# A scale for the value weights as a whole, the spatial product in float16 pairs, and masked key products evicted by another engine

## The chip, the cores and the metric

The kernel runs on one core of a Trainium2 chip. Its engines work through queues of their own: TensorE (PE: matmuls and transposes, with weight loads that overlap them), VectorE (DVE), ScalarE (ACT), GpSimd (POOL) and SyncE (SP, which here only issues DMAs). An engine takes its instructions in order and waits on semaphores for the others. Matmul results land in PSUM, of which there are eight banks, and are read from there by DVE or ACT. The metric is the device time of one execution in microseconds (us); lower is better.

## What is computed

One layer of a backbone with three parallel branches over 2048 + 128 tokens of width 1024. All inputs are float32. Cut to what the change touches:

```python
proj = einsum('btd,de->bte', xn, w_in)          # one projection, split into the branches' columns
# A: delta rule over chunks of 64 tokens
m = eye + beta[..., :, None] * einsum('bnhik,bnhjk->bnhij', k, k) * dec_strict
# B: spatial gating over chunks of 128 tokens, 4 groups of 128 channels
vn = rmsnorm(v, g_norm)                         # over 512 channels
vs = einsum('gpq,bnqgc->bnpgc', w_s, vn) + b_s  # w_s: (4, 128, 128)
o_b = u * vs * silu(z_b)
# C: Fourier mixing; then the branches' projections, sigmoid gates and the output projection
```

Here v is one of the column blocks of the projection, 512 wide, and the spatial product mixes the 128 tokens of a chunk within each group of channels.

## The kernel before

**Pairs of float16.** Almost every product is made from float16 pairs: an operand x with a scale s (a power of two) is kept as hi = f16(x s) and lo = f16(x s - hi), and the product is hi hi + hi lo + lo hi, three matmuls that add up in PSUM (`mm3`, `gemm_T`, `gemm_N`). ACT makes the high half, DVE the low one. The scale comes from a sum of squares: ACT squares and sums along a partition, a matmul with ones (`scales`) sums across partitions, and four one-column steps on DVE turn the sum's exponent into s and its inverse.

**Weights** are read by SP into one of two buffers (`wst`) and converted by a generator, `converting`, of which `weight_step` runs one step at each tick of the pacing object `pace`; `getw` takes the next weights of a list, `wlist`, and runs the remaining steps at once if they aren't done. The four column blocks of v have the tag "v" and fill one pair of tiles, `v4`; each block has its own scale and its own inverse.

**Order of the work.** After the input's normalisation come twelve tiles of the q, k and v columns of branch A (the loop over `ct`, line 610): matmuls over five token blocks, evicted by ACT into `raw`, a short convolution by three DVE instructions into `cy` (626 to 628), a SiLU by ACT and POOL (631, 632), and a store to DRAM (`qkv`, line 633). These tiles live in a pool `a1p`, which is closed behind the loop (639).

Then branch B begins (1131). It opens a pool `bp`, loads the bias `bsp`, transposes the spatial weights `wsn` into `wsT` (float32, line 1141), and runs over 17 blocks of 128 tokens (1159): 24 matmuls of xh, xl with `v4` into a bank of the PSUM pool `ps_mm` (three banks, in turn); line 1168 evicts it by DVE, with each block's inverse scale, into `vn` (a tile "sg" of the pool `ep`); ACT sums its squares into `vss` (1171, a tile of `bp`); DVE and POOL make the reciprocal root (170, 171); DVE scales `vn` by it (1177). One block later, `spatial` multiplies `vn` with `wsT` in float32, four groups into one bank of `ps_x` (two banks), and four DVE instructions (1151) apply the weight of the norm, which stands along partitions there (`sgug`), and add the bias. The result goes to DRAM and is read back by the loop over the gates (1191).

**Beside the branches** runs branch A's recurrence, a generator `delta` of which `pace.tick` runs a step after every so many microseconds of matmuls. Its first part, `prep` (677), makes for each of the 17 chunks the key product k k^T (729), and for both directions masks it: four DVE instructions per direction (735) multiply a head's 128x128 block in PSUM by beta and the decay. ACT copies the diagonal blocks (737) and makes the high half (739), DVE the low half (740). `base_inverse` (762) inverts the small diagonal blocks on DVE. All of `prep` reads what line 633 stored.

The instructions' order on each engine is set by a scheduler at build time, from the program's order and a timing model; dependences become semaphores.

Of the kernel before, what the change touches and what calls it, by code (L numbers as in the profile page):

```python
# [111 lines left out]
def hybrid_flow_kernel(ctx: ExitStack, tc: tile.TileContext, x_prompt, x_sample, state_delta, c, c_ctx, ln_g, w_ada,  # L112
# [85 lines left out]
    def converting(w, st, nkt, cols=P, hi=None, lo=None, tag="w", bufs=5):  # L198

        wpool = bwp[0] if tag == "b" else wp  # L200
        if tag == "z":
            hi, lo = [sb(p0p, [P, nkt, cols], n_, F16, bufs=4) for n_ in ("zhi", "zlo")]
        if tag == "v":
            hi, lo = [t[:, vfilled[0]] for t in v4]
            vfilled[0] += 1
        w.hi = sb(wpool, [P, nkt, cols], tag + "hi", F16, bufs=bufs) if hi is None else hi
        w.lo = sb(wpool, [P, nkt, cols], tag + "lo", F16, bufs=bufs) if lo is None else lo
        ss = sb(wp, [P, 1], "wss", bufs=4)
        A.activation(w.lo, st, AF.Square, accum_out=ss)  # L209
# [12 lines left out]
        A.activation(w.hi, st, AF.Copy, scale=s)  # L222
        V.scalar_tensor_tensor(w.lo, st, s, w.hi, ALU.mult, ALU.subtract)  # L223
# [33 lines left out]
    for c0 in ([C_QKV + i * P for i in range(12)] + [C_V + g * P for g in range(4)]  # L257
               + [x_ + g * P for g in range(4) for x_ in (C_U, C_ZB)] + [x_ + g * P for g in range(4) for x_ in (C_XC, C_ZC)]):
        wlist.append((w_in_[:, c0:c0 + P], KT, "v" if C_V <= c0 < C_V + WB else "w", 4))
# [4 lines left out]
    v4, vfilled = [], [0]  # L264
    goal = [0]
    wdone, wnext, wread, wlate, bwp, wsteps = [], [0], [], [0], [], []

# [340 lines left out]
    flip = [0]  # L608
    pace.start(decays(), 1.2)
    for ct in range(12):  # L610
        w = getw(1, 2 if ct < 6 else min(4, 15 - ct))
        for half in range(1):
            raw = sb(a1p, [P, LP], "raw")
            G.memset(raw[:, 0:1], 0.0)
            G.memset(raw[:, NS + 1:NS + 3], 0.0)
            G.memset(raw[:, LP - 1:LP], 0.0)
            for t0, tn in TBS:
                flip[0] ^= 1
                ps = bank(ps_d if flip[0] else ps_mm, [P, tn])
                gemm_T(ps, w, 0, xh[:, :, t0:t0 + tn], xl[:, :, t0:t0 + tn])  # L620
                o = t0 + 1 if t0 < NS else t0 + 3
                with tc.high_priority():
                    A.activation(raw[:, o:o + tn], ps, AF.Copy, scale=w.inv)
                pace.tick(tn / 100)
            y = sb(a1p, [P, LP - 2], "cy")
            V.tensor_scalar(y, raw[:, 0:LP - 2], convw(0, ct), None, ALU.mult)
            V.scalar_tensor_tensor(y, raw[:, 1:LP - 1], convw(1, ct), y, ALU.mult, ALU.add)
            V.scalar_tensor_tensor(y, raw[:, 2:LP], convw(2, ct), y, ALU.mult, ALU.add)
            for c0 in range(0, LP - 2, CQ):
                c1 = min(c0 + CQ, LP - 2)  # L630
                A.activation(raw[:, 1 + c0:1 + c1], y[:, c0:c1], AF.Sigmoid)  # L631
                G.tensor_tensor(y[:, c0:c1], y[:, c0:c1], raw[:, 1 + c0:1 + c1], ALU.mult)  # L632
            G.dma_start(qkvD[ct], y)
            if ct < 4 or ct > 7:
                A.activation(raw[:, 1:LP - 1], y, AF.Square, accum_out=vqs[:, ct:ct + 1])
# [41 lines left out]
    def prep(g, ci, t, nxt, held):  # L677
# [54 lines left out]
        for d in range(2):  # L732
            n_ = sb(d2, [P, WB], "n32", bufs=3)
            for h in range(H):
                V.scalar_tensor_tensor(n_[:, hs(h)], ps[:, hs(h)], beta[:, d, t, h:h + 1], dc[:, d, hs(h)], ALU.mult, ALU.mult)
# [3 lines left out]
            A.activation(n16[:, 0, :], n_, AF.Copy, scale=FS)  # L739
            V.scalar_tensor_tensor(n16[:, 1, :], n_, FS, n16[:, 0, :], ALU.mult, ALU.subtract)  # L740
            late(nD[d][t], n16)
            yield 1
# [390 lines left out]
    bp = pool(bs, "bp", 2)  # L1133
    bsp = sb(bp, [P, 4, P], "bsp", bufs=1)
    SY.dma_start(bsp, b_spatial[0].rearrange("g (o p) -> o g p", o=1).to_broadcast([P, 4, P]))
# [5 lines left out]
    V.tensor_copy(wsT, ps)  # L1141
    vinv = sb(ep, [P, 4], "vinv", bufs=1)
    for i in range(4):
        V.tensor_copy(vinv[:, i:i + 1], vw[i].inv)
    def spatial(t, vn):
        vs = sb(bp, [P, 4, P], "vs", bufs=4)
        ps = bank(ps_x, [P, 4, P])
        for g in range(4):
            mm(ps[:, g, :], vn[:, g, :], wsT[:, g, :])
        for g in range(4):  # L1150
            V.scalar_tensor_tensor(vs[:, g, :], ps[:, g, :], sgug(g), bsp[:, g, :], ALU.mult, ALU.add)
        vout.append((t, vs))

    def vstore():
# [4 lines left out]
    for t in range(NCH):  # L1159
        ps = bank(ps_mm, [P, 4, P])  # L1160
        ts = slice(t * P, (t + 1) * P)
        for k in range(KT):
            mm(ps, xh[:, k, ts], v4[0][:, :, k, :], k == 0, False)
            mm(ps, xh[:, k, ts], v4[1][:, :, k, :], False, False)
            mm(ps, xl[:, k, ts], v4[0][:, :, k, :], False, k == KT - 1)
        vn = sb(ep, [P, WB], "sg", bufs=4).rearrange("p (i c) -> p i c", i=4)
        with tc.high_priority():
            V.tensor_tensor(vn, ps, vinv.rearrange("p (i o) -> p i o", o=1).to_broadcast([P, 4, P]), ALU.mult)
        sq = sb(ep, [P, WB], "st", bufs=3)
        ss = sb(bp, [P, 1], "vss", bufs=3)  # L1170
        A.activation(sq, vn.rearrange("p i c -> p (i c)"), AF.Square, accum_out=ss)
        rsqrt(ss, ss, 1.0 / WB, 1)
        if vprev is not None:
            spatial(*vprev)
        if len(vout) > 2:
            vstore()
        V.tensor_scalar(vn, vn, ss, None, ALU.mult)
# [354 lines left out]
```

## Time and profile before

| | |
|---|---|
| time, median of 3 runs | 2209.3 us (2206.56 to 2211.78) |
| the profiled execution, first to last instruction | 2205.0 us |
| time around that span, by the median | 4.3 us |
| granted TensorE clock, mean | 0.993 |
| HBM read, written | 234.67 MB, 127.62 MB |

The profile is one execution; the page gives its span, and the median of the runs is 4.3 us above it. A row of instructions gives line, engine, operation, what is written and read, shape and count, then the busy time in us and the mean of one in ns, then the engine's idle time ahead of them and what ended it. A matmul's recorded duration holds its way through the array, so that the next one starts before it ends: what one costs is read from the distance of the starts. A row of stages gives the busy time of each engine within a window of the span. The granted clock is the share of full speed that the throttle gave TensorE.

### The profile page before, as it was taken

The page shows a single profiled execution, that of the slowest core. Times are in us where ns is not written, and L with a number is a line of the kernel's source. Part 1 is how long each engine was busy: PE and PEld are TensorE (multiplying, and loading weights), DVE is VectorE, ACT ScalarE, POOL GpSimd, SP SyncE. Part 2 cuts the span into 40 slices and gives each one's busy share as a digit, 9 for nine tenths or more (in the row PEclk, how much of TensorE's full clock was granted, in tenths as well). Part 3 has the DMA queues.
Part 4 walks back from the last instruction along what each step waited for, and adds up shares of the span by engine and source line. Part 5 has one row for each costly group of instructions (what it writes and reads, how often), then busy time and mean ns, then how long its engine had stood idle before and what let it go on. Part 6 is the DMA issues. An engine that isn't in the chain of part 4 may idle for free. (4 is left out here: it accounts for less than half of the span.)

```text
span 2205.0 us, 42035 instructions
## 1 busy us (share of the span) xinstructions
PE 2139.0 (97%) x15966; PEld 1233.8 (56%) x15966; DVE 1295.6 (59%) x3081; ACT 1007.0 (46%) x2322; POOL 704.9 (32%) x860
## 2 busy tenths in 40 slices
PE   7999999999999999999999999999999999999998
PEld 3564444456555588878555555556554444444443
DVE  5736954479889778255665555765674544223454
ACT  3644744445465464344644445665553422222332
POOL 1421333223343322432322223354542221122543
PEclk9999999999999999999999999999999999999999
DMA  8434823177786662443665555776664544324542
GB/s 280 143 96 147 287 94 107 63 210 221 232 245 221 203 186 88 116 122 114 220 182 162 163 167 183 238 212 213 193 197 151 168 127 131 117 77 125 170 149 103
DMA packets 304276, 365.05 MB, mean 166 GB/s; under 512 B 39393, under 2 KB 215626, under 8 KB 302026
## 3 DMA queue, kind: packets, MB, share of 16 engines
q1 hardware_dynamic: 288938, 302.19, 45.5%
q0 software_dynamic: 12688, 51.27, 6.4%
q10 hardware_dynamic: 2448, 8.91, 1.0%
q8 instruction: 125, 2.05, 0.4%
q14 instruction: 77, 0.63, 0.1%
HBM read 234.67 MB, written 127.62 MB: 164 GB/s over the span
## 5 line engine op out<-in xcount | busy, mean ns | idle before, releaser
L161 PE MATMUL b<-xh,whi 128*128 128x512 f16 (+1 forms) x1920 | 650.4, 347 | 3.2 <-DVE mrow L1361 1.2
L161 PE MATMUL b<-xl,whi 128*128 128x512 f16 (+1 forms) x1920 | 650.9, 347 | 0.0
L161 PE MATMUL b<-xh,wlo 128*128 128x512 f16 (+1 forms) x1920 | 650.4, 347 | 0.0
L161 PEld LDWEIGHTS <-whi 128*128 128x128 f16 x3904 | 358.1, 98 | 328.8 <-issue 7.9
L161 PEld LDWEIGHTS <-wlo 128*128 128x128 f16 x1952 | 191.3, 98 | 179.8 <-issue 2.4
L161 PE MATMUL b<-big,bhi 128*128 128x512 f16 (+1 forms) x960 | 251.6, 348 | 2.2 <-ACT big L1325 1.5
L1365 POOL TENSOR_TENSOR mrow<-mrow,sg 128x512 f32<-128x512 f32 (+1 forms) x80 | 91.9, 1149 | 296.5 <-DVE sg L1364 216.3
L161 PE MATMUL b<-big,blo 128*128 128x512 f16 (+1 forms) x480 | 163.7, 348 | 0.0
L1355 ACT ACTIVATE sg<-b,winv 128x512 f32<-128x512 f32 (+1 forms) x120 | 74.2, 618 | 170.5 <-PE b L161 169.6
L161 PEld LDWEIGHTS <-xh 128*128 128x128 f16 x1496 | 117.6, 98 | 30.2 <-issue 1.5
L161 PEld LDWEIGHTS <-bhi 128*128 128x128 f16 x960 | 86.7, 98 | 73.1 <-issue 2.7
L1364 DVE SCALAR_TENSOR_TENSOR sg<-b,binv,sg 128x512 f32<-128x512 f32 (+1 forms) x80 | 53.4, 668 | 125.2 <-PE b L161 118.1
L632 POOL TENSOR_TENSOR cy<-cy,raw 128x545 f32<-128x545 f32 (+1 forms) x48 | 66.9, 1421 | 183.4 <-ACT raw L631 183.4
L175 DVE CAST wscb<-wss 128x1 bf16<-128x1 f32 x93 | 14.3, 154 | 154.7 <-ACT wlo L209 65.8
L852 POOL COPY T<-ES 32x256 f16<-32x256 f16 x68 | 32.3, 475 | 207.1 <-DMA ES<-ei 168.2
L161 PE MATMUL b<-wlo,xh 128*128 128x128 f16 x544 | 92.9, 219 | 0.0
L161 PE MATMUL b<-whi,xh 128*128 128x128 f16 x544 | 92.9, 219 | 0.0
L161 PE MATMUL b<-whi,xl 128*128 128x128 f16 x544 | 92.9, 219 | 0.0
L161 PE MATMUL b<-wohi,mh 128*128 128x512 f16 x240 | 90.9, 379 | 1.3 <-ACT mh L1432 1.3
L161 PE MATMUL b<-wohi,ml 128*128 128x512 f16 x240 | 90.8, 379 | 0.3 <-DVE ml L1433 0.3
L161 PE MATMUL b<-wolo,mh 128*128 128x512 f16 x240 | 90.9, 379 | 0.0
L223 DVE SCALAR_TENSOR_TENSOR wlo<-wst,wsc,whi 128x1024 f16<-128x1024 f32 x52 | 70.4, 1358 | 30.8 <-ACT whi L222 30.7
(449 smaller groups left out, 4284.0 us busy)
## 6 DMA issues: line engine op xcount, KB each, us to landing
wst<-in_w_in_dram SPq DMA_DIRECT2D x60, 512.0 KB
qkv<-cy POOLq DMA_DIRECT2D x12, 1089.0 KB, 5.3
st<-br SPq DMA_DIRECT2D x48, 256.0 KB
mrow<-mrg SPq DMA_DIRECT2D x18, 512.0 KB
mrow<-mrg SPq DMA_DIRECT2D x16, 576.0 KB
mrg<-mrow POOLq DMA_DIRECT2D x16, 576.0 KB, 3.6
dc<-dec SPq DMA_DIRECT2D x17, 512.0 KB
kq<-qkv SPq DMA_DIRECT2D x34, 256.0 KB
```

The lines of the kernel that those rows point to most:

```text
L161: PE.matmul(out, l, r, start=start, stop=stop)
L175: V.tensor_copy(sb16, ss)
L223: V.scalar_tensor_tensor(w.lo, st, s, w.hi, ALU.mult, ALU.subtract)
L632: G.tensor_tensor(y[:, c0:c1], y[:, c0:c1], raw[:, 1 + c0:1 + c1], ALU.mult)
L852: G.tensor_copy(T16[rows(a0, b), :, :, b], ES[0:32, :, 2 * a0 + b, :, wT])
L1355: A.activation(sg, ps, AF.Sigmoid, scale=gw.inv)
L1364: V.scalar_tensor_tensor(sg, ps, binv[:, 1:2], sg, ALU.mult, ALU.mult)
L1365: G.tensor_tensor(mr, mr, sg, ALU.add)
```

## The change

In words, by part:

- **Value weights.** Each of the four blocks stands twice in the list. With tag "p" (a probe) it is read and its squares are summed into a column of `vsq`; after the fourth, one scale for all four is made. With tag "v" it is read again and converted with that scale. `getw` takes eight entries in place of four, and the convolution loop asks for more entries ahead (8 from tile 8 on).
- **Setup of branch B.** The weight of the norm is loaded as a row, `grow`, broadcast to all partitions, and multiplied by the inverse scale of v, by a scale for itself and by 1/64. `gss`, `grow`, `w16`, `einv` and `v16` are tiles of `bp`. The spatial weights become a float16 pair, `w16`, with a scale.
- **Eviction.** ACT squares and sums straight out of PSUM, with the inverse scale; DVE multiplies PSUM by `grow` into `vn`.
- **Product.** ACT and DVE make `vn` times the reciprocal root into a float16 pair, `v16`; the spatial product is three float16 matmuls per group; one DVE instruction over all four groups scales it and adds the bias. `vs` has three buffers in place of four.
- **Masked key products.** ACT evicts the four heads with beta as its scale, and one DVE multiplication over all heads applies the decay.

```diff
@@ converting
+        if tag == "p":
+            i = len(vprobed)
+            vprobed.append(i)
+            A.activation(v4[1][:, i], st, AF.Square, accum_out=vsq[:, i:i + 1])
+            yield
+            if i == 3:
+                V.tensor_reduce(vsq[:, 4:5], vsq[:, 0:4], AX.X, ALU.add)
+                vscale.extend(scales(vsq[:, 4:5], cp, "vsc"))
+                V.tensor_mul(vsq[:, 5:6], vscale[1], isx)
+            return
         if tag == "v":
             hi, lo = [t[:, vfilled[0]] for t in v4]
             vfilled[0] += 1
+            A.activation(hi, st, AF.Copy, scale=vscale[0])
+            V.scalar_tensor_tensor(lo, st, vscale[0], hi, ALU.mult, ALU.subtract)
+            return
@@ wlist
+    for tag in "pv":
+        for g in range(4):
+            wlist.append((w_in_[:, C_V + g * P:C_V + (g + 1) * P], KT, tag, 4))
@@ convolution loop
-        w = getw(1, 2 if ct < 6 else min(4, 15 - ct))
+        w = getw(1, 2 if ct < 6 else 4 if ct < 8 else 8)
@@ prep
             for h in range(H):
-                V.scalar_tensor_tensor(n_[:, hs(h)], ps[:, hs(h)], beta[:, d, t, h:h + 1], dc[:, d, hs(h)], ALU.mult, ALU.mult)
+                A.activation(n_[:, hs(h)], ps[:, hs(h)], AF.Copy, scale=beta[:, d, t, h:h + 1])
+            V.tensor_mul(n_, n_, dc[:, d, :])
@@ branch B
-    wsT = sb(bp, [P, 4, P], "wsT", bufs=1)
-    vw = getw(4, 3)
+    grow = sb(bp, [P, WB], "grow", bufs=1)
+    SY.dma_start(grow, sgu_norm_g.to_broadcast([P, WB]))
+    w16 = sb(bp, [P, 2, 4, P], "w16", F16, bufs=1)
+    vw = getw(8, 3)
+    gss = sb(bp, [P, 2], "gss", bufs=1)
+    junk = sb(ep, [P, WB], "sg", bufs=4)
+    A.activation(junk[:, 0:4], pc[:, 44:48], AF.Square, accum_out=gss[:, 0:1])
+    A.activation(junk, wsn.rearrange("p g q -> p (g q)"), AF.Square, accum_out=gss[:, 1:2])
+    sg_, ig_ = scales(gss[:, 0:1], bp, "gsc")
+    sw_, iw_ = scales(gss[:, 1:2], bp, "ssc")
+    vinv = vsq[:, 5:6]
+    V.tensor_scalar(grow, grow, vinv, sg_, ALU.mult, ALU.mult)
+    V.tensor_scalar(grow, grow, 1.0 / 64, None, ALU.mult)
+    einv = sb(bp, [P, 1], "einv", bufs=1)
+    V.scalar_tensor_tensor(einv, ig_, 64.0, iw_, ALU.mult, ALU.mult)
     ps = bank(ps_x, [P, 4, P])
     for g in range(4):
         PE.transpose(ps[:, g, :], wsn[:, g, :], ident)
-    V.tensor_copy(wsT, ps)
...
+    A.activation(w16[:, 0], ps, AF.Copy, scale=sw_)
+    V.scalar_tensor_tensor(w16[:, 1], ps, sw_, w16[:, 0], ALU.mult, ALU.subtract)
@@ spatial
         for g in range(4):
-            mm(ps[:, g, :], vn[:, g, :], wsT[:, g, :])
-        for g in range(4):
-            V.scalar_tensor_tensor(vs[:, g, :], ps[:, g, :], sgug(g), bsp[:, g, :], ALU.mult, ALU.add)
+            mm3(ps[:, g, :], [v16[:, l, g * P:(g + 1) * P] for l in range(2)], [w16[:, l, g, :] for l in range(2)])
+        V.scalar_tensor_tensor(vs, ps, einv, bsp, ALU.mult, ALU.add)
@@ loop over 17 blocks
         with tc.high_priority():
-            V.tensor_tensor(vn, ps, vinv.rearrange("p (i o) -> p i o", o=1).to_broadcast([P, 4, P]), ALU.mult)
...
-        A.activation(sq, vn.rearrange("p i c -> p (i c)"), AF.Square, accum_out=ss)
+            A.activation(sq, psf, AF.Square, scale=vinv, accum_out=ss)
+            V.tensor_mul(vn, psf, grow)
         rsqrt(ss, ss, 1.0 / WB, 1)
...
-        V.tensor_scalar(vn, vn, ss, None, ALU.mult)
-        vprev = (t, vn)
+        v16 = sb(bp, [P, 2, WB], "v16", F16)
+        A.activation(v16[:, 0, :], vn, AF.Copy, scale=ss)
+        V.scalar_tensor_tensor(v16[:, 1, :], vn, ss, v16[:, 0, :], ALU.mult, ALU.subtract)
+        vprev = (t, v16)
```

More of the change, by code (lines that the diff above doesn't have):

```diff
@@ L256, in hybrid_flow_kernel @@
         wlist.append((w_in_[:, c0:c0 + P], KT, "z", 4))
-    for c0 in ([C_QKV + i * P for i in range(12)] + [C_V + g * P for g in range(4)]
-               + [x_ + g * P for g in range(4) for x_ in (C_U, C_ZB)] + [x_ + g * P for g in range(4) for x_ in (C_XC, C_ZC)]):
-        wlist.append((w_in_[:, c0:c0 + P], KT, "v" if C_V <= c0 < C_V + WB else "w", 4))
+    for i in range(12):
+        wlist.append((w_in_[:, C_QKV + i * P:C_QKV + (i + 1) * P], KT, "w", 4))
+    for tag in "pv":
+        for g in range(4):
+            wlist.append((w_in_[:, C_V + g * P:C_V + (g + 1) * P], KT, tag, 4))
+    for c0 in ([x_ + g * P for g in range(4) for x_ in (C_U, C_ZB)] + [x_ + g * P for g in range(4) for x_ in (C_XC, C_ZC)]):
+        wlist.append((w_in_[:, c0:c0 + P], KT, "w", 4))
     for n in (1, 2, 0):
@@ L1140, in hybrid_flow_kernel, with spatial @@
         PE.transpose(ps[:, g, :], wsn[:, g, :], ident)
[L1141 to L1146, printed above, removed]
+    A.activation(w16[:, 0], ps, AF.Copy, scale=sw_)
+    V.scalar_tensor_tensor(w16[:, 1], ps, sw_, w16[:, 0], ALU.mult, ALU.subtract)
+    def spatial(t, v16):
+        vs = sb(bp, [P, 4, P], "vs", bufs=3)
         ps = bank(ps_x, [P, 4, P])
         for g in range(4):
-            mm(ps[:, g, :], vn[:, g, :], wsT[:, g, :])
-        for g in range(4):
-            V.scalar_tensor_tensor(vs[:, g, :], ps[:, g, :], sgug(g), bsp[:, g, :], ALU.mult, ALU.add)
+            mm3(ps[:, g, :], [v16[:, l, g * P:(g + 1) * P] for l in range(2)], [w16[:, l, g, :] for l in range(2)])
+        V.scalar_tensor_tensor(vs, ps, einv, bsp, ALU.mult, ALU.add)
         vout.append((t, vs))
@@ L1165, in hybrid_flow_kernel @@
             mm(ps, xl[:, k, ts], v4[0][:, :, k, :], False, k == KT - 1)
-        vn = sb(ep, [P, WB], "sg", bufs=4).rearrange("p (i c) -> p i c", i=4)
-        with tc.high_priority():
-            V.tensor_tensor(vn, ps, vinv.rearrange("p (i o) -> p i o", o=1).to_broadcast([P, 4, P]), ALU.mult)
+        psf = ps.rearrange("p i c -> p (i c)")
+        vn = sb(ep, [P, WB], "sg", bufs=4)
         sq = sb(ep, [P, WB], "st", bufs=3)
         ss = sb(bp, [P, 1], "vss", bufs=3)
-        A.activation(sq, vn.rearrange("p i c -> p (i c)"), AF.Square, accum_out=ss)
+        with tc.high_priority():
+            A.activation(sq, psf, AF.Square, scale=vinv, accum_out=ss)
+            V.tensor_mul(vn, psf, grow)
         rsqrt(ss, ss, 1.0 / WB, 1)
```

5 lines of the change are left out of this document (3 added, 2 removed).

## The prediction, made before the change was run

> **What bounds the kernel now.** I read the page first, then the busy time by stage, then who TensorE (PE) waited for, then the timeline of the two places that the diff touches.
>
> ```profile
> span 2205.0 us, 42035 instructions
> PE 2139.0 (97%) x15966; PEld 1233.8 (56%) x15966; DVE 1295.6 (59%) x3081; ACT 1007.0 (46%) x2322; POOL 704.9 (32%) x860
> ```
> PE is busy for 97% of the span, so the kernel is a stream of matmuls in a fixed order. Time goes away only where PE gets less to do or waits less, and any new wait of PE is added nearly whole. The whole idle time of PE is 66 us.
>
> ```profile
> 355.00:427.00 72.00, 72.00 (x410) 35.66 (x409) 28.65 (x42) 32.93 (x49) 17.40 (x26) 1.00 0.30 99
> ...
> 427.00:460.00 33.00, 33.00 (x180) 17.84 (x178) 18.99 (x48) 12.64 (x36) 10.30 (x13) 1.00 0.45 130
> 460.00:560.00 100.00, 97.63 (x625) 58.95 (x624) 89.66 (x267) 52.56 (x165) 29.92 (x41) 1.00 0.68 207
> 560.00:700.00 140.00, 134.73 (x849) 75.77 (x847) 117.73 (x284) 80.66 (x247) 52.68 (x63) 0.99 0.79 244
> 700.00:850.00 150.00, 143.66 (x1381) 104.87 (x1379) 116.57 (x289) 88.88 (x263) 54.71 (x69) 0.99 0.62 188
> ```
> Each row has a stage's length, the busy time of PE, PE's weight loads, DVE, ACT and POOL (instructions in brackets), the granted clock, the DMA engines' share and GB/s. These are the stages that the diff touches: the end of the convolution loop, where the value weights are converted (355 to 427), the start of the spatial branch (427 to 460), the rest of it (to 560), and the preparation of the key products, which runs beside all branch work to about 850. In the first two PE doesn't stop at all. After 460 VectorE (DVE) is the fullest helper (324 of 390 us), ScalarE (ACT) has 222.
>
> ```profile
> PE b L161 <- DVE T L721: 6.1, 3, 2.8
> PE b L719 <- DVE tok L703: 2.1, 2, 1.9
> PE b L686 <- DVE n L735: 1.8, 2, 1.2
> PE b L161 <- DVE sg L1177: 1.2, 1, 1.2
> PE b L161 <- DVE sg L1115: 1.2, 1, 1.2
> PE b L161 <- ACT T L720: 1.1, 2, 0.9
> ```
> The waits of PE from 427 to 850 (total, times, longest): 12.4 us for DVE, 1.1 for ACT's T. That is all that a lighter DVE can give back there.
>
> **Part 1, the product in float16 pairs: less work for PE.** Timeline of PE; an x counts merged records, and the next row's start tells when they were through:
>
> ```profile
> 457.12 1.95 PE L161 MATMUL b<-wsT,sg 128*128 128x128 f32 x16
> 458.91 0.38 PE L161 MATMUL b<-v4lo,xh 128*128 128x512 f16 x1
> ...
> 839.11 0.67 PE L161 MATMUL b<-q,T 128*128 128x128 f16 x9
> 839.61 0.22 PE L161 MATMUL b<-xh,whi 128*128 128x128 f16 x1
> ```
> A float32 product of 128x128 leaves two records (136 for 68 products); 16 take 458.91 - 457.12 = 1.79 us, so 112 ns each and 8 x 112 = 0.90 us for a token block. In float16 nine take 0.50 us, 55.6 ns each; twelve (four groups by three products) make 0.67 us. Saved: 0.23 us a block, 17 blocks, **-3.9 us**. The scale products of single columns (four go, three come) are under 0.1 us.
>
> **Part 2, the first eviction waits for memory: a new stall.** The tiles of the spatial branch's own pool lie where the convolution's buffers lay. Timelines of PE, POOL, DVE, SP's queue and ACT at its start:
>
> ```profile
> 427.35 0.38 PE L161 MATMUL b<-v4hi,xh 128*128 128x512 f16 x1
> 433.96 0.69 DVE L1168 TENSOR_TENSOR sg<-b,vinv 128x512 f32<-128x512 f32 x1
> 439.64 0.60 POOL L633 DMA_DIRECT2D qkv<-cy  x1 [0.30 <-POOL cy L632]
> 442.92 0.38 PE L161 MATMUL b<-v4hi,xh 128*128 128x512 f16 x1
> 444.12 0.69 DVE L1141 COPY wsT<-b 128x512 f32<-128x512 f32 x1 [0.31 <-DMA qkv<-cy]
> 444.32 0.34 SPq L1135 DMA_DIRECT2D bsp<-in_b_spatial_dram  x1
> 444.39 0.63 ACT L1171 ACTIVATE st<-sg 128x512 f32<-128x512 f32 x1 [2.89 <-DMA qkv<-cy]
> ```
> The last store of the convolution is issued at 439.64 and lands near 444.1. Three tiles of the new pool (wsT, the sum vss, bsp) are first written right then, on three engines: the pool is free only when that store has landed. Today nothing on PE's path minds: the PSUM of block 0 is read at 433.96 by L1168, whose operands (vinv, sg) lie in another pool. After the change PSUM is read by a multiplication with grow and by a Square that sums into vss, both in the late pool. PE has three banks for these blocks; it fills them from about 426.9 (the four transposes that stand before 427.35, 0.44 us, move behind the scales) to 442.5, and block 3, at 442.92 today, must wait for block 0's bank. I see no other ready work: the key preparation waits for the same store, and later branches use the same banks in turn.
>
> When is the bank free? Grow's load follows bsp's on SP's queue, so it is issued 0.34 us later, at about 444.7; the key loads behind it move back by one issue. No row has its landing; the nearest with one are stores:
>
> ```profile
> kv<-tok POOLq DMA_DIRECT2D x17, 512.0 KB, 5.5
> mrg<-mrow POOLq DMA_DIRECT2D x16, 512.0 KB, 3.2
> ```
> bsp and grow together are 512 KB as well. I take 3.2, since little else moves at 444: 447.9. Then come two multiplications of grow by scales, for which L1177 is the nearest row, and the one out of PSUM, as long as L1168's 0.69 above:
>
> ```profile
> L1177 DVE TENSOR_SCALAR sg<-sg,vss 128x512 f32<-128x512 f32 x17 | 8.2, 483 | 1.8 <-POOL vss L171 1.6
> ```
> 2 x 0.48 + 0.69 + some 0.2 of hand-over gives 449.8. The scale chain for g (a small Square after 444.1, cast, product, four one-column steps; about 2 us in all) ends before grow lands. PE stands from 442.5 to 449.8, 7.3 us, less the 0.44 us of transposes that it does meanwhile: **+6.9 us**. Ends: 5.0 if the load were instant and the scale chain alone decided, 9.2 with a landing of 5.5. No gain is possible, for PE has no idle here today.
>
> A stall of that length has a tail. Busy time and granted clock around two gaps of today (columns as above):
>
> ```profile
> 705.00:710.00 5.00, 3.97 (x38) 2.64 (x37) 4.66 (x16) 0.60 (x1) 1.86 (x3) 1.00 0.94 342
> 710.00:715.00 5.00, 4.10 (x49) 4.09 (x49) 3.78 (x5) 4.72 (x6) 0.00 (x0) 0.72 0.18 68
> 715.00:720.00 5.00, 5.00 (x25) 2.59 (x24) 5.00 (x18) 4.94 (x19) 3.87 (x6) 0.94 0.66 103
> 890.00:895.00 5.00, 0.87 (x9) 0.68 (x7) 1.68 (x3) 1.56 (x4) 5.00 (x7) 0.81 0.96 312
> 895.00:900.00 5.00, 3.74 (x16) 3.48 (x17) 2.70 (x6) 2.26 (x7) 1.90 (x5) 0.51 0.54 111
> ```
> After the idle 1.9 us near 709 the clock is 0.72, then 0.94: 5 x 0.28 + 5 x 0.06 = 1.7 us of clock lost. After the idle 4 us near 892 it is 0.51 for a whole stretch, 5 x 0.49 = 2.4 lost. I take **+1.7 us**; ends 0 and 3.4.
>
> The Trainium skill, "TensorE: Matmul & The Clock Gate", Part 1 (the HAM clock gate), has the clock halve after an idle window of about 3.4 us and recover after as long a busy one, the windows running freely. By it a stall of 7 us always halves the clock, and at half speed one to two windows would lose an estimated 1.7 to 3.4 us: the sum below, or 1.7 more. The trace is harsher than the page, since already 1.9 us of idle is followed by 0.72.
>
> **Part 3, work moved from DVE to ACT: nearly nothing.**
>
> ```profile
> L735 DVE SCALAR_TENSOR_TENSOR n<-b,beta,dc 128x128 f32<-128x128 f32 x136 | 36.9, 343 | 2.0 <-PE b L161 2.0
> L750 DVE TENSOR_TENSOR n<-b,dc 128x512 f32<-128x512 f32 x34 | 22.9, 684 | 2.1 <-PE b L161 2.1
> L740 DVE SCALAR_TENSOR_TENSOR n<-n,n 128x512 f16<-128x512 f32 x34 | 23.3, 688 | 6.0 <-ACT n L739 5.7
> L1151 DVE SCALAR_TENSOR_TENSOR vs<-b,pc,bsp 128x128 f32<-128x128 f32 x68 | 19.7, 343 | 0.0
> L905 ACT ACTIVATE o<-b,eg 128x128 f32<-128x128 f32 x128 | 36.7, 368 | 30.3 <-DMA br<-o 16.0 <-PE b L161 14.2
> ```
> Masked key products: DVE loses L735's 36.9 us and gains 34 wide multiplications like L750's (22.9): -14. ACT gains 136 evictions like L905's: 36.7 x 136/128 = +39. Spatial branch: DVE loses L1151 (19.7) and L1177 (8.2) and gains 17 low halves like L740's (0.69) and 17 wide evictions (0.69 too): -4.5; ACT gains 17 high halves like L1171's 0.63 above: +10.7. So DVE falls by 18.5 of its 324 us, 6%, and ACT rises from 222 to 272 of 390. If PE's 12.4 us behind DVE shrink in proportion, 0.7; with a little of the clock lost after such gaps, **-1 us**. Ends: -14 (all these waits and the clock lost near 709 go) and +2 (the waits behind ACT more than double). The key product's bank is free as early as before: eight evictions take 8 x 0.287 = 2.3 us on ACT against 8 x 0.271 = 2.2 on DVE.
>
> **Part 4, the weights read twice: nothing.** Four more reads of 512 KB go to SP's queue between 355 and 427, where the DMA engines are 30% busy. Counting steps of the converter (two ticks for a probe, one for a conversion), the last conversion falls on the first tick of the last convolution tile, about 20 us before the branch begins; the number of Squares stays. The cover is that loop, where PE is busy 72.00 of 72.00 us. If it failed, the branch would start with a read of 3.2 to 5.5 us and a conversion.
>
> **Sum.** -3.9 + 6.9 + 1.7 - 1.0 = +3.7 us on the profiled span: 2208.7. The runs' median of 2209.3 is 4.3 above that span; with the same 4.3, **2213.0 us**. A measurement of this kernel can tell about 0.2%, 4.4 us, from no change.
>
> **Rivals.** *No stall* (the new pool's grow and vss lie in a part freed early, or the scheduler finds other work): -3.9 - 1 = -4.9, 2204.4. Against it: three tiles of the pool, on three engines, waited for the same landing. This is also the way in which the f16 saving would show alone. *Relief*: the stall comes, but DVE's waits nearly all go, -3.9 + 8.6 - 10 = -5.3, 2204.0. For it: L721's 6.1 us are DVE queueing behind other work; against it: only 6% of that queue goes. *ACT late* (slower): between a block's product and its spatial product now stand Square, its sum, the power on POOL, an ACT high half and a DVE low half, about 3 us, within the 5.2 us of the next block (24 products). ACT also takes the key evictions in bursts of 1.1 us and silu evictions. If its queue is over 2.2 us late, PE waits in each block; 0.5 us in 16 blocks is 8: 2221. For it: such a wait stands already (L1177, 1.2 us); against it: one in 17, and ACT at 70% at most. The Trainium skill, "ScalarE: Activation LUTs", Rules for kernel authors, advises multiplications on VectorE; the row agrees mildly, 368 ns on ACT for 343 on DVE.
>
> **Chances.** Forecast (its own range 2209 to 2217) 0.55, of which 0.22 is slower by over 4.4 us, 0.33 within; no stall 0.16, 0.12 faster and 0.04 within; relief 0.11, 0.07 and 0.04; ACT late 0.18, slower. Together: faster 0.19, within 0.41, slower 0.40. The range takes in both fast rivals and the start of the slow one's: 2203 to 2221.
>
> **What would show it.** A gap of PE of 5 to 9 us near 442.5, ended by DVE's multiplication out of PSUM, and a clock of about 0.5 behind it; spatial products at 0.67 us a block; L735's rows on ACT near 0.37 each; the waits behind L721 about as now. If PE runs on at 443, Part 2 is wrong; if the waits after 460 differ from 13 us by more than 5, Part 3 is.

## The result and the profile after

| | before | after |
|---|---|---|
| time, median of 9 runs each | 2207.5 us (2205.1 to 2211.8) | 2223.0 us (2210.4 to 2230.5) |
| ratio to before, 95% interval | | 1.0061 [1.0043, 1.0078] |
| the profiled execution, first to last instruction | 2205.0 us | 2222.1 us |
| granted TensorE clock, mean | 0.993 | 0.988 |

The change makes the kernel slower by 0.6%; of some 2204 us that is 13.5 us (9.5 to 17). The forecast had +3.7. The runs of after lie 20 us apart, those of before 7, so the ratio carries more than any single pair of times. The first lines of the page after:

```profile
span 2222.1 us, 42144 instructions
PE 2144.2 (96%) x16033; PEld 1234.1 (56%) x16033; DVE 1281.9 (58%) x2920; ACT 1052.9 (47%) x2480; POOL 705.9 (32%) x860
```

PE's busy time rose by 5 us although its product became shorter; work at a low clock is busy for longer (a product of 128x512 starts every 0.43 us at half clock near 459, every 0.22 at full clock behind 461). So I cut both traces at the same marks of the work. In the view by stage a row has the stage, its length, the busy times of PE, PE's weight loads, DVE, ACT and POOL with their instructions, the granted clock, the DMA share and GB/s. The marks are PE's first product with the value weights, the first product of the loop over the gates and the start of the Fourier branch. Before:

```profile
427.10:549.60 122.50, 120.13 (x731) 70.69 (x730) 99.80 (x287) 60.81 (x190) 37.79 (x49) 1.00 0.64 196
549.60:788.70 239.10, 227.84 (x1652) 137.20 (x1650) 198.28 (x492) 136.58 (x414) 90.20 (x111) 0.99 0.73 224
```

After:

```profile
200.00:430.70 230.70, 227.73 (x1249) 110.79 (x1247) 134.88 (x132) 121.77 (x173) 74.27 (x87) 0.99 0.48 161
430.70:564.20 133.50, 123.18 (x821) 70.31 (x819) 101.34 (x240) 84.96 (x253) 40.58 (x52) 0.95 0.62 187
564.20:809.80 245.60, 229.94 (x1640) 136.59 (x1638) 188.50 (x413) 155.34 (x494) 86.90 (x108) 0.97 0.69 214
```

The time came in three stages: 3.6 us before the spatial branch (430.7 for 427.1), 11.0 in it (133.5 for 122.5, clock 0.95), 6.5 behind it, where the key products are prepared beside the gates (245.6 for 239.1, clock 0.97 for 0.99). Together 21.1 us, more than the 17.1 between the spans: stages that the change doesn't touch came out 4 us shorter in this execution.

**In the spatial branch: the stall that was forecast.** Timelines of PE, DVE and SP's queue after:

```profile
446.28 0.38 PE L161 MATMUL b<-v4hi,xl 128*128 128x512 f16 x1
450.32 0.16 PE L161 MATMUL b<-gscb,ones 128*128 128x1 bf16 x1 [3.66 <-DVE gscb L175]
454.44 1.11 PE L704 MATMUL b<-cst,kq 128*128 128x128 f32 x4 [3.95 <-DMA kq<-qkv]
...
453.49 0.55 DVE L1166 TENSOR_SCALAR grow<-grow,vsq,gsc 128x512 f32<-128x512 f32 x1 [2.37 <-DMA grow<-in_sgu_norm_g_dram]
454.54 1.88 DVE L1202 TENSOR_TENSOR sg<-b,grow 128x512 f32<-128x512 f32 x3
...
448.77 0.43 SPq L1156 DMA_DIRECT2D grow<-in_sgu_norm_g_dram  x1
```

PE stops after three blocks and stands for 3.66 + 3.95 = 7.6 us, in two halves. The first ends with the scale product of the norm's weight. The second is put down to the key load, since PE's order has key transposes next; but the eviction L1202 also starts only at 454.54, so PE had nothing else either way. The eviction waited for grow: issued at 448.77, used at 453.49, 4.7 us later. The clock then stays low:

```profile
450.00:451.00 1.00, 0.16 (x1) 0.00 (x0) 0.68 (x7) 1.00 (x4) 0.68 (x2) 0.61 0.90 219
...
459.00:460.00 1.00, 1.00 (x4) 0.32 (x3) 1.00 (x2) 0.00 (x0) 0.00 (x0) 0.50 0.71 206
460.00:461.00 1.00, 1.00 (x5) 0.39 (x4) 0.06 (x1) 0.00 (x0) 0.00 (x0) 0.77 0.00 0
461.00:462.00 1.00, 1.00 (x8) 0.72 (x7) 0.00 (x0) 0.00 (x0) 0.00 (x0) 1.00 0.00 0
```

It is 0.50 from about 450.2 to 460.5. PE is at work from 454.4 on, so it loses half of 6.1 us: 3 us beside the 7.6.

**Before the branch: a gap that was not forecast.** Timelines of ACT near 340 us, first before:

```profile
339.01 1.05 ACT L209 ACTIVATE wlo<-wst 128x1024 f16<-128x1024 f32 x1
...
345.06 1.06 ACT L209 ACTIVATE v4lo<-wst 128x1024 f16<-128x1024 f32 x1 [4.91 <-DMA wst<-in_w_in_dram]
```

After, with PE's row and the two windows around it:

```profile
344.49 1.06 ACT L206 ACTIVATE v4lo<-wst 128x1024 f16<-128x1024 f32 x1 [7.09 <-DMA wst<-in_w_in_dram]
...
345.80 1.04 ACT L222 ACTIVATE wlo<-wst 128x1024 f16<-128x1024 f32 x1
```

```profile
347.46 0.16 PE L161 MATMUL b<-wscb,ones 128*128 128x1 bf16 x1 [2.97 <-DVE wscb L175]
```

```profile
345.00:350.00 5.00, 2.54 (x8) 0.98 (x8) 3.91 (x4) 2.21 (x6) 0.00 (x0) 0.78 0.40 105
350.00:355.00 5.00, 5.00 (x22) 2.11 (x21) 3.06 (x6) 1.66 (x4) 0.00 (x0) 0.88 0.39 105
```

The Square of the last convolution weight (written to `wlo`) stood at 339.01. After the change the first probe's Square (written to `v4lo`) is ahead of it in ACT's queue and waits 7.09 us for its read, so the convolution weight is squared only at 345.80. PE's next work is that weight's scale product: 2.97 us of idle PE, and 5 x 0.22 + 5 x 0.12 = 1.7 us of clock.

**Behind the branch** no single gap stands out. PE's waits from 427 to 850 after (total, times, longest):

```profile
PE b L161 <- DVE T L739: 4.6, 5, 1.6
PE b L737 <- DVE tok L721: 4.1, 3, 3.3
...
PE b L161 <- ACT T L738: 2.0, 1, 2.0
```

The waits behind these two of DVE's tiles, 8.2 before (6.1 and 2.1), are 8.7, though DVE got lighter; the wait behind ACT's T is 2.0 for 1.1. The rows by stage have it as many small pieces: from the first gate product to the Fourier branch PE is idle for 15.7 us in place of 11.3, and by the trace's clock record the clock is halved for 13.7 us in place of 6.8.

### The profile page after: what moved, and what is told of

It reads as the page before. It is cut to its first block, busy times and chain, and to the rows that moved or that the text cites. A ratio compares the mean times of both kernels' runs of the same rounds, so it can differ in the third digit from the quotient of the medians.

```text
span 2222.1 us, 42144 instructions
## 1 busy us (share of the span) xinstructions
PE 2144.2 (96%) x16033; PEld 1234.1 (56%) x16033; DVE 1281.9 (58%) x2920; ACT 1052.9 (47%) x2480; POOL 705.9 (32%) x860
## 5 line engine op out<-in xcount | busy, mean ns | idle before, releaser
L175 DVE CAST wscb<-wss 128x1 bf16<-128x1 f32 x89 | 13.7, 154 | 133.6 <-ACT wlo L222 62.6
```

What stands on the lines that cost most here:

```text
L175: V.tensor_copy(sb16, ss)
```

## The experiments

Ratios are to the kernel before, with its 95% interval. Differences between two runs are differences of their ratios times 2204 us; their half-widths add the two intervals' half-widths as squares.

### The stall, reading the weights once, and the key part

**e1_pool**: the changed kernel with what the first evictions need in a small pool that is opened ahead of the convolution loop.

```diff
+    bq = pool(v4s, "bq", 1)
...
-    grow = sb(bp, [P, WB], "grow", bufs=1)
+    grow = sb(bq, [P, WB], "grow", bufs=1)
...
-        ss = sb(bp, [P, 1], "vss", bufs=3)
+        ss = sb(bq, [P, 1], "vss", bufs=3)
```

(`gss`, `einv` and the tiles of both scales move likewise.)

> The changed kernel with grow, the three one-column scales and sums and vss in a pool opened ahead of the convolution loop, so that they don't wait for its last store; nothing else. Theory (the first evictions wait for the late pool): PE's idle of 7.6 us at 446 to 454 and most of the half clock behind it (some 3 us) go, about 2213 us (2210 to 2216) against 2223 for the changed kernel. Rival (PE would stand anyway, since the key loads wait for the same store and come next in its order): at least half of the gap stays, 2218 or more.

Measured: 2209.14 us, 1.0024 [1.0011, 1.0038], 8.2 (+-4.9) us less than after. Its windows where after stood:

```profile
445.00:450.00 5.00, 5.00 (x25) 2.28 (x24) 1.16 (x5) 2.80 (x4) 2.30 (x4) 1.00 0.46 192
450.00:455.00 5.00, 5.00 (x25) 2.29 (x24) 2.82 (x5) 2.51 (x5) 0.56 (x1) 1.00 0.47 118
```

PE runs through at full clock. The place of those tiles was the cause of the stall, and taking it away gives 8 us. By the traces it cost somewhat more, 7.6 + 3 us; but the gap before the branch is 2 us dearer in e1_pool's execution (5.5 us idle and 1.3 of clock, where the changed kernel has 3.0 and 1.7).

**e2_noprobe**: the changed kernel reads each value weight once; the scale comes from a constant sum.

```diff
-    for tag in "pv":
-        for g in range(4):
-            wlist.append((w_in_[:, C_V + g * P:C_V + (g + 1) * P], KT, tag, 4))
+    for g in range(4):
+        wlist.append((w_in_[:, C_V + g * P:C_V + (g + 1) * P], KT, "v", 4))
...
+        G.memset(vsq[:, 4:5], 4.0)
+        vscale.extend(scales(vsq[:, 4:5], cp, "vsc"))
...
-        w = getw(1, 2 if ct < 6 else 4 if ct < 8 else 8)
+        w = getw(1, 2 if ct < 6 else min(4, 15 - ct))
```

> The changed kernel without the four probe reads: the scale of the value weights is made from a constant, 4.0 a partition, in place of their squares, and the look-ahead is that of before. Leaves out the sum of squares of the value weights. Theory (a probe's Square, waiting for its read, stood on ACT ahead of the Square of the last convolution weight, and PE waited 3.0 us for that weight's scale at 344, with a slow clock behind it): 4 to 5 us faster than the changed kernel, about 2218.5. Rival (the gap at 344 is an accident of the run, or the reads cost nothing): 2223, within 2.

Measured: 2217.72 us, 1.0064 [1.0046, 1.0082]: no gain, a miss. The gap before the branch was still there, 4.85 us. ACT's timeline says why:

```profile
346.98 1.15 ACT L216 ACTIVATE v4hi<-wst,vsc 128x1024 f16<-128x1024 f32 x1 [7.37 <-DMA wst<-in_w_in_dram]
...
348.29 1.04 ACT L222 ACTIVATE wlo<-wst 128x1024 f16<-128x1024 f32 x1
```

There is no probe any more, but now the first conversion of a value weight stands ahead of the convolution weight's Square, and waits for its read in the same way. Not the second reading, but a waiting instruction placed ahead of a needed one, became the theory.

**e3_nokey** is the changed kernel with the key products as before, **e4_key** the kernel before with the new key products alone (the diff is that of e4_key; e3_nokey is it reversed):

```diff
             for h in range(H):
-                V.scalar_tensor_tensor(n_[:, hs(h)], ps[:, hs(h)], beta[:, d, t, h:h + 1], dc[:, d, hs(h)], ALU.mult, ALU.mult)
+                A.activation(n_[:, hs(h)], ps[:, hs(h)], AF.Copy, scale=beta[:, d, t, h:h + 1])
+            V.tensor_mul(n_, n_, dc[:, d, :])
```

> The changed kernel with the masked key products evicted as before (four DVE instructions a direction, none on ACT). Theory (key evictions on ACT make PE wait: its idle from 460 to 850 rose from 14.0 to 18.4 us, and its clock fell): 4 to 7 us faster than the changed kernel, 2216 to 2219. Rival (that part costs nothing, as predicted, and the rise comes from the spatial branch): 2223, within 2.

> The kernel before with the key products' part of the change alone. Theory (ACT late): 4 to 7 us slower than before, about 2212 to 2214. As predicted (nearly nothing): within 2 us of before, about 2206.5.

Measured: e3_nokey 2210.36 us, 1.0033 [1.0020, 1.0046], so the key part costs 6.2 (+-4.8) us within the changed kernel; e4_key 2214.19 us, 1.0051 [1.0035, 1.0067], 11 us alone. "Nearly nothing" is refuted on the slower side. The profiled execution of e4_key was the fastest of its six (2206.7), so its trace understates the price; still the stage of the gates shows 246.8 us for 239.1:

```profile
549.20:796.00 246.80, 229.51 (x1636) 135.38 (x1635) 191.79 (x423) 157.08 (x500) 88.91 (x111) 0.98 0.70 214
```

### ACT's order, the product, and a first try at ACT's load

**e6_order**: e1_pool with the probe's Square tied behind the last convolution weight's.

```diff
-            A.activation(v4[1][:, i], st, AF.Square, accum_out=vsq[:, i:i + 1])
+            with tc.issue_after(lastsq[0].ins):
+                A.activation(v4[1][:, i], st, AF.Square, accum_out=vsq[:, i:i + 1])
...
-        A.activation(w.lo, st, AF.Square, accum_out=ss)
+        lastsq[:] = [A.activation(w.lo, st, AF.Square, accum_out=ss)]
```

> The kernel of run e1_pool (the stall at the branch's start is gone there), with the Square of a probed value weight issued behind the Square of the last convolution weight on ScalarE. Theory 1, the order on ScalarE makes the gap near 344 us (a Square that waits for a weight's read stands ahead of an eviction and of the last convolution weight's Square): the gap, 5.5 us of idle PE in e1_pool and about 1.7 us of clock behind it, goes, so 5 to 7 us less than e1_pool: a ratio near 1.000 to the kernel before. Rival: the gap only shows a conversion that is late for another reason (the reads share the DMA engines): it stays or moves by a few us, and the time is within 2 us of e1_pool (1.0024).

Measured: 2203.25 us, 0.9996 [0.9986, 1.0005], 6.2 (+-3.6) us below e1_pool. ACT's timeline and the windows:

```profile
340.78 1.06 ACT L223 ACTIVATE wlo<-wst 128x1024 f16<-128x1024 f32 x1
...
348.03 1.06 ACT L207 ACTIVATE v4lo<-wst 128x1024 f16<-128x1024 f32 x1 [6.09 <-DMA wst<-in_w_in_dram]
```

```profile
345.00:350.00 5.00, 5.00 (x26) 2.29 (x25) 3.74 (x7) 1.15 (x2) 0.00 (x0) 1.00 0.44 126
```

The probe still waits 6 us for its read, but nothing that PE needs stands behind it, and the gap is gone. Its read landed no earlier (348.03 for 344.49 after); the order alone was the cause.

**e7_order_nokey**: e6_order with the key products as before (the diff of e4_key, reversed).

> Run e6_order with the masked key products evicted by VectorE as before the change. Theory 1, the key part costs by itself wherever it stands (6 us in e3_nokey against the changed kernel, 11 us in e4_key against the kernel before): 6 to 11 us less than e6_order, a ratio of 0.995 to 0.997, faster than both kernels. Rival: the key part's price was the luck of two schedules: within 2 us of e6_order.

Measured: 2200.35 us, 0.9984 [0.9974, 0.9994], the fastest of the kernels that compute all. The key part costs 2.6 (+-3.0) us here, less than expected and not told from nothing; so its price hangs on the schedule around it.

**e9_f32**: e7_order_nokey with the spatial product in float32.

```diff
-            mm3(ps[:, g, :], [v16[:, l, g * P:(g + 1) * P] for l in range(2)], [w16[:, l, g, :] for l in range(2)])
+            mm(ps[:, g, :], v16[:, g * P:(g + 1) * P], w16[:, g, :])
...
-        v16 = sb(bp, [P, 2, WB], "v16", F16)
-        A.activation(v16[:, 0, :], vn, AF.Copy, scale=ss)
-        V.scalar_tensor_tensor(v16[:, 1, :], vn, ss, v16[:, 0, :], ALU.mult, ALU.subtract)
+        v16 = vn
+        V.tensor_scalar(vn, vn, ss, None, ALU.mult)
```

(`w16` becomes one float32 tile, made by one ACT instruction.)

> Run e7_order_nokey with the spatial product in float32 as before (VectorE scales vn, no pairs; the one scale, the row factors and the single last instruction stay). Theory 1, the product in pairs saves PE 0.23 us in each of 17 blocks and nothing else changes: 3.9 us more than e7_order_nokey, 0.0018 of the ratio. Rival: the saving is eaten by the pair's two conversions between a block and its spatial product: within 1 us, or less time than e7_order_nokey.

Measured: 2206.02 us, 1.0011 [0.9998, 1.0023], 6.0 (+-3.5) us above e7_order_nokey. The saving of the pairs is real; 3.9 lies in that interval.

**e8_actload**: the kernel before with extra evictions by ACT from the same bank.

```diff
+            jk = sb(d2, [P, WB], "jk", bufs=1)
             for h in range(H):
+                A.activation(jk[:, hs(h)], ps[:, hs(h)], AF.Copy, scale=beta[:, d, t, h:h + 1])
                 V.scalar_tensor_tensor(n_[:, hs(h)], ps[:, hs(h)], beta[:, d, t, h:h + 1], dc[:, d, hs(h)], ALU.mult, ALU.mult)
```

> The kernel before, with its key products on VectorE as they were, and four more evictions per direction by ScalarE out of the same bank into a tile that nobody reads: ScalarE gets the 39 us that the key part moved to it, and no chain runs through them but the bank. Theory 1, ScalarE's load is what costs (its other work comes late by the burst): 7 to 11 us more than the kernel before, a ratio of 1.003 to 1.005, and waits behind T by ScalarE as in e4_key. Rival: the chain from ScalarE to VectorE and back, or the order that it gives VectorE's instructions, is what costs: within 2 us of the kernel before.

Measured: 2224.46 us, 1.0085 [1.0071, 1.0099], 19 us, twice the expectation. The rows by line from 549 to 790 show that more than a load was added:

```profile
L736 ACT ACTIVATE jk<-b,beta 128x128 f32<-128x128 f32 x76 | 27.8, 366 | 62.9 <-DVE n L737 58.8 <-PE b L161 3.8
```

The last columns are ACT's idle time ahead of these instructions and what ended it: 58.8 us behind DVE's evictions of the same bank. The two engines took turns. This run doesn't measure a load, and it doesn't decide its question.

### The key part taken apart

**e10_actsb**: the same extra work for ACT, without the bank. **e11_relief**: DVE's relief without ACT's load; the first head's beta stands for all four. **e12_chain**: the key part in the other order.

```diff
@@ e10_actsb
+            jk = sb(d2, [P, WB], "jk", bufs=1)
+            for h in range(H):
+                A.activation(jk[:, hs(h)], dc[:, d, hs(h)], AF.Copy, scale=beta[:, d, t, h:h + 1])
@@ e11_relief, in place of the four of a direction
+            V.scalar_tensor_tensor(n_, ps, beta[:, d, t, 0:1], dc[:, d, :], ALU.mult, ALU.mult)
@@ e12_chain, likewise
+            V.tensor_mul(n_, ps, dc[:, d, :])
+            for h in range(H):
+                A.activation(n_[:, hs(h)], n_[:, hs(h)], AF.Copy, scale=beta[:, d, t, h:h + 1])
```

> The kernel before, with four more evictions' worth of ScalarE work per direction at the place of the key products, but read from the decay rows in SBUF and written to a tile that nobody reads: ScalarE's load of the key part alone (39 us), without a bank and without a hand-over to VectorE. In e8_actload the extra evictions waited in turn with VectorE's for the bank, which this leaves out. Theory 1, ScalarE's load is the price of the key part: 8 to 14 us more than the kernel before (1.004 to 1.006), PE's waits behind T and tok up in the stage from 549 to 790 us. Rival, the price lies in the order and the hand-over of the key products: within 3 us of the kernel before.

> The kernel before, with the four evictions of a direction by VectorE made one over all heads, with the first head's beta for all four (the beta of the other heads is left out): VectorE's relief by the key part alone, 14 us of its load, and ScalarE as before. My prediction's step: 1 us less at the most likely, an end of 14. Theory 1, VectorE's queue holds PE: 4 to 10 us less (0.995 to 0.998). Rival, VectorE's load isn't what PE waits for but its order: within 2 us of the kernel before.

> The key part alone on the kernel before, in the other order: VectorE applies the decay to all heads out of the bank first, then ScalarE applies beta per head in SBUF, where its copies and the high half follow. Loads of both engines as in e4_key (1.0051), but one hand-over from ScalarE to VectorE and back is gone, and the bank is free after one instruction. Theory 1, ScalarE's load is the price: as e4_key, 1.003 to 1.007. Rival, the hand-over is: within 3 us of the kernel before, or faster.

Measured: e10_actsb 2213.26 us, 1.0054 [1.0038, 1.0069], +12 us; e11_relief 2195.52 us, 0.9967 [0.9955, 0.9979], -7.3 us; e12_chain 2213.34 us, 1.0044 [1.0032, 1.0056], +9.7 us. The stretch that the prediction summed, 460 to 850, first before, then e10_actsb, then e11_relief:

```profile
460.00:850.00 390.00, 376.02 (x2851) 239.59 (x2850) 323.96 (x838) 222.10 (x672) 137.31 (x172) 0.99 0.70 213
```

```profile
460.00:850.00 390.00, 368.85 (x2653) 228.31 (x2652) 310.86 (x820) 249.65 (x775) 128.75 (x163) 0.98 0.68 206
```

```profile
460.00:850.00 390.00, 379.30 (x2946) 242.52 (x2944) 316.53 (x752) 222.68 (x673) 139.17 (x171) 1.00 0.69 213
```

PE's idle time is the first number less the second: 14.0, 21.2 and 10.7 us. The clock is 0.99, 0.98 and 1.00; by the traces' clock records it is halved for 6.8, 13.7 and 0 us, and half of that is lost. Idle time and clock together give 7.2 + 3.4 = 10.6 us more in e10_actsb and 3.3 + 3.4 = 6.7 less in e11_relief, nearly what the runs show, so the effects do lie in this stretch, and a third to a half of each is clock. The key part holds two effects of opposite sign, a gain of 7 and a price of 12 or more, and I had put both near nothing. These two don't add up to it, though: 12 - 7 = 5, and e4_key costs 11, so e10_actsb doesn't hold the whole price, or the two effects don't simply add. DVE's rows give the relief its size: L735's 36.9 us became, in e11_relief,

```profile
L734 DVE SCALAR_TENSOR_TENSOR n<-b,beta,dc 128x512 f32<-128x512 f32 x34 | 23.8, 743 | 2.1 <-PE b L161 2.0
```

13 us less of DVE's work gave 7.3 (+-2.6) us of time. By the medians more than half of what DVE sheds at this place was time on PE's path.

The ACT side is less clean. The view of the added line in e10_actsb has this under idle time ahead of it:

```profile
  DMA dc<-dec: 42.0, 15
```

The added instructions also waited for the decay rows, and held ACT's queue. Who then waited is seen in DVE's own waits from 460 to 850 (total, times, longest), first before, then e10_actsb:

```profile
DVE n L740 <- ACT n L739: 5.7, 9, 1.1
```

```profile
DVE ss L693 <- ACT sq L692: 15.2, 15, 2.4
...
DVE n L743 <- ACT n L742: 7.5, 12, 1.4
```

(The first of these is 2.0 before.) DVE makes its halves and sums behind ACT's, so a late ACT can make DVE late, and DVE is what PE waits for most. e4_key has the low half behind the high half (in before L740 behind L739, 5.7) at twice that; but so has e11_relief, which is the faster one. First e4_key, then e11_relief:

```profile
DVE n L741 <- ACT n L740: 11.5, 15, 1.3
```

```profile
DVE n L739 <- ACT n L738: 12.9, 12, 1.9
```

So a longer wait of DVE behind ACT is not by itself the price, and that the price comes about in this way is argued, not shown. Of PE's own waits in e10_actsb, the one behind ACT's T rose from 1.1 to 4.2 us and the one behind DVE's T fell from 6.1 to 3.1.

The hand-over that e12_chain takes away gave no gain that these intervals show (1.0044 against 1.0051). What ACT's 39 us cost in the key part itself follows by difference, if the two effects add up: 11 + 7 = 18 us alone, 6 + 7 = 13 in the changed kernel, 3 + 7 = 10 in the mended one.

**e13_pooldec**: e7_order_nokey with beta applied to the decay rows by POOL ahead of time, so that DVE gets the relief and ACT no load.

```diff
+        bd = [sb(d2, [P, WB], "n32", bufs=3) for d in range(2)]
+        for d in range(2):
+            G.tensor_tensor(h3(bd[d]), h3(dc[:, d, :]), bc(beta[:, d, t, :], P), ALU.mult)
...
-            n_ = sb(d2, [P, WB], "n32", bufs=3)
-            for h in range(H):
-                V.scalar_tensor_tensor(n_[:, hs(h)], ps[:, hs(h)], beta[:, d, t, h:h + 1], dc[:, d, hs(h)], ALU.mult, ALU.mult)
+            n_ = bd[d]
+            V.tensor_mul(n_, ps, n_)
```

> Run e7_order_nokey with beta applied to the decay rows by GpSimd (34 multiplications of 128x512 in SBUF, about 1.17 us each by e7's rows, 40 us on an engine that is 32% busy), and one wide multiplication per direction by VectorE out of the bank. VectorE gets the relief of e11_relief, ScalarE gets no load. Theory 1, VectorE's relief is worth what e11_relief showed wherever the work goes off PE's path: 5 to 8 us less than e7_order_nokey, a ratio of 0.995 to 0.996, the fastest of all. Rival, the added work is on the path whichever engine takes it (GpSimd also makes the reciprocal roots and the gates' products that PE's order waits for): within 2 us of e7_order_nokey, or slower.

Measured: 2204.09 us, 1.0003 [0.9994, 1.0013], 4.2 (+-3.0) us above e7_order_nokey: a miss. Its groups of POOL and DVE from 440 and 460 to 850:

```profile
L738 POOL TENSOR_TENSOR n<-dc,beta 128x512 f32<-128x512 f32 x34 | 38.9, 1148 | 24.8 <-DVE n L775 17.5 <-DVE n L762 5.4 <-DVE wsc L186 1.3
...
L775 DVE SCALAR_TENSOR_TENSOR n<-n,n 128x512 f16<-128x512 f32 x33 | 27.5, 842 | 4.5 <-ACT n L774 4.5
```

POOL stood 24.8 us ahead of the new work, mostly until DVE had freed a buffer of `n32`, which the early product now holds longer. DVE's low half took 842 ns on the mean where it took 693 in e7_order_nokey. Which of the two ate the relief was not tried.

## Why the prediction was right and where it was wrong

Taken off the changed kernel one after the other, the parts come to: stall 8.2 (e1_pool), order on ACT 6.2 (e6_order), key products 2.6 (e7_order_nokey), and what stays is -3.5 us against before: 8.2 + 6.2 + 2.6 - 3.5 = 13.5. The sum of the prediction was 6.9 + 1.7 - 1.0 - 3.9 + 0 = 3.7, of which the stall and the product held and the other two did not.

- **Part 1, the product: right.** Twelve float16 products take 0.67 us in after (464.03 - 463.36), eight of float32 0.89 in e9_f32 (458.85 - 457.96), as worked out:

```profile
463.36 0.83 PE L161 MATMUL b<-w,v 128*128 128x128 f16 x12
464.03 0.39 PE L737 MATMUL b<-cst,tok 128*128 128x128 f32 x2
```

```profile
457.96 1.05 PE L161 MATMUL b<-w,sg 128*128 128x128 f32 x8
458.85 0.38 PE L161 MATMUL b<-v4hi,xh 128*128 128x512 f16 x1
```

  The whole kernel gave 6.0 (+-3.5) for it. The rival *ACT late*, a wait in each block for the pair's conversions, did not come: the stay of -3.5 us in e7_order_nokey leaves no room for its 8, and PE's waits behind the pair's high half are two there, 1.4 us in all. That ACT's queue can hold PE, its premise, came true in the key products (e10_actsb, 12 us).
- **Part 2, the stall: right in place, mechanism and nearly in size.** Predicted 6.9 idle and 1.7 of clock, 8.6; the trace has 7.6 and 3, the chip 8.2 when it is taken out (net of a dearer gap before the branch, as said at e1_pool). Grow took 4.7 us and not 3.2; the end that I allowed was 5.5. I looked for one gap ended by DVE's multiplication; it was two, named after a scale and a key load. *No stall* fell with it.
- **Part 3, the key products: wrong, and it is the step "if PE's 12.4 us behind DVE shrink in proportion, 0.7".** The loads moved as summed (DVE 304 us in the stretch for 305.5 worked out; L753 on ACT at 0.38). But DVE's 13 us at this place are worth 7.3, not 0.7, and the same work on ACT costs more than that, 10 to 18 by difference. I priced ACT's rise at nothing because ACT was at most 70% busy; a share says nothing on whether ACT's instruction is the next that DVE needs. My ends, -14 to +2, hold neither 6 nor 11; the 2.6 (+-3.0) of the mended kernel they don't exclude. That the term as a whole missed by only 4 to 7 us is luck, since two larger errors of opposite sign cancelled in part. The mark that I set, waits that differ from 13 us by more than 5, is just passed by the 18.4 us of idle PE from 460 to 850, and just not if they are set against the 14.0 before: it was too coarse, and it left out the clock. *Relief* was right on what DVE's time is worth, and wrong in that it forgot ACT's side.
- **Part 4, the weights read twice: wrong, 6.2 us, in the word "nothing".** I asked only when the value weights are ready, and that held: the last of their conversions starts on DVE at 401.3 us after, 29 us before the branch. What failed was an earlier step. "The number of Squares stays" says nothing of their order: the new first step of the list, a Square that waits for a read, was put ahead of another weight's Square in ACT's queue. Nor was it the second reading as such, since e2_noprobe reads once and has the gap too. The cover that I named, a PE that is busy 72.00 of 72.00 us, begins at 355; the gap lies at 344, outside the rows that I read.

That 2213 was too low by some 10 us is thus two terms: 6 us for the order on ACT and 4 to 7 for the key products. The measured 2223.0 lies 2 above the range's end; 1.0061 times the earlier 2209.3 gives the same.

Left open: what part of ACT's price in the key products is load and what the order that it forces (both loads that I added brought a wait of their own), and why it falls from 11 us alone to 3 in the mended kernel. Open too is why the order made at build time put the waiting Square ahead.

## What to carry to other kernels

A step that is moved or added is priced in each queue that it enters: look at what stands behind its wait there, above all in the stage ahead of the one that the change is about. Tiles that the first instructions of a stage need belong in memory that is free by then; a pool that reuses the last stage's buffers makes them wait for that stage's last store. Work that is moved from a full helper to an idle one is two changes, a gain and a price; measure each by itself, since here both were far above what shares of busy time had suggested.

## What the hardware showed beside that

The half clock after the stall lasted from about 450.2 to 460.5 us, 10.3 us, though PE was at work again for the last 6. In e1_pool, around its gap at 344 (5.5 us of idle PE), it lasted from about 349.2 to 352.6, 3.4 us:

```profile
349.00:350.00 1.00, 0.03 (x2) 0.03 (x2) 1.00 (x3) 0.44 (x2) 0.00 (x0) 0.60 0.65 147
350.00:351.00 1.00, 1.00 (x4) 0.40 (x4) 1.00 (x1) 0.00 (x0) 0.00 (x0) 0.50 1.14 345
...
352.00:353.00 1.00, 1.00 (x5) 0.41 (x4) 0.90 (x2) 1.00 (x3) 0.00 (x0) 0.70 0.00 0
353.00:354.00 1.00, 1.00 (x6) 0.48 (x5) 1.00 (x1) 0.54 (x1) 0.00 (x0) 1.00 0.00 0
```

The clock was halved only near the end of that gap, so that a gap of 5.5 us lost less clock (some 1.3 us of work) than the split one of 7.6 (3 us), and less than the gap of 2.97 us near 344 after (1.7 us). The Trainium skill, "TensorE: Matmul & The Clock Gate", Part 1 (the HAM clock gate), has the clock set by windows of 3.4 us that run freely; both stretches agree, one window here and three there. That such a window must be idle for the clock to halve, as the prediction has it from there, does not hold here: a gap of 2.97 us was enough.

How much is enough can be read off the traces. Between 100 and 2100 us the fourteen of them have 76 stretches of half clock; each lasts one, two or three times 3.41 us, and those of one trace lie on one grid. Cut along that grid, PE was busy for at most 53% of the window ahead of each stretch, and for at least 45% of every window behind which a full clock stayed full. The full clock came back behind windows of 77% or more. The two ends are e4_key, where the clock was halved behind 1.79 of 3.41 us, and e9_f32, where it was not behind 1.57 of 3.42:

```profile
1385.38:1388.79 3.41, 1.79 (x25) 1.06 (x22) 2.88 (x4) 2.14 (x5) 1.33 (x1) 1.00 0.38 120
1388.79:1392.21 3.42, 3.42 (x24) 2.36 (x22) 2.91 (x12) 2.97 (x6) 0.00 (x0) 0.50 0.64 161
```

```profile
710.37:713.79 3.42, 1.57 (x19) 1.04 (x17) 1.71 (x2) 3.42 (x4) 0.41 (x2) 1.00 0.16 59
713.79:717.20 3.41, 2.44 (x41) 2.32 (x42) 3.41 (x6) 1.70 (x3) 1.73 (x3) 1.00 0.18 28
```

So some 1.6 to 1.9 us of idle PE within one window are what it takes in these traces, in one gap or in several, and a halved window that PE fills costs 1.7 us more. What a stall costs beyond itself thus depends on where it lies in the windows, and can't be read from its length.
